# State space operands made in 27 steps between a network's half groups, and u laid out by parts with copies

## The chip, the cores and the metric

The kernel runs on one core of one Trainium2 chip. The metric is the device time of one execution in microseconds; the time before is the median of 3 runs. On this core TensorE (PE) multiplies, VectorE (DVE), ScalarE (ACT) and GpSimd (POOL) work on elements, and SyncE (SP) issues the transfers (DMAs). Each engine takes its instructions in the order in which they stand in its queue.

## The reference, cut to what matters

A sequence of 256 tokens of width 1024 goes through two hybrid layers (a gated delta rule mixer and a gated feed forward network) and then through two layers of another kind, each of three parts: network, token mixer, network. The change lies in the second kind. Its token mixer has a state space branch:

```python
lam_bar = jnp.exp(lam * dt)                          # 32 groups x 64 states, complex
b_bar = ((lam_bar - 1.0) / lam)[..., None] * b
bu = jnp.einsum('blgn,gpn->blgp', uf.astype(jnp.complex64), b_bar)
_, states = lax.associative_scan(combine, (a_all, bu), axis=1)   # state = lam_bar * state + bu
y = jnp.real(jnp.einsum('gnp,blgp->blgn', c, states)) + d_skip * uf
...
def swiglu(h, w_in, w_out):                          # the networks around it
    gate, up = jnp.split(h @ w_in, 2, axis=-1)
    return (jax.nn.silu(gate) * up) @ w_out
```

The kernel doesn't scan token by token. It takes four tokens at a time (SL = 4) and needs, per layer, matrices that depend on the weights alone: the input weights times the powers of lam_bar, the output weights times the powers, their products among the four tokens, and a table of powers. These are the state space operands of the title.

## The kernel before, in words

All tokens stay on the chip and all weights stream in once. Every product is made in three f32 parts: each weight block of 128x1024 is fetched by SP (`wr`, 512 KB, 4 buffers), cast by ACT or by DVE (L232, L234) to `wh` (5 buffers), and DVE subtracts the two to give `wl` (L241, 4 buffers). `wblk` keeps four blocks ahead: while the matmuls of block n are written, the fetch, cast and subtraction of block n + 4 are.

A network (`ffn`) goes through its hidden columns in groups of four tiles of 128 (g0 = 0, 4, ..., 20). Per group there are two half groups, gate and up. Each half group (`group`) is four weight blocks and 96 matmuls of 128x256 in L271; a block holds two of the eight steps of the contraction for all four tiles, so that all four sums open in the first block of the half group and close in its last. The sums lie in the PSUM pool `pg`, which has four banks. An up half group takes over the gate's banks when ACT has made `sg` of them (L432), and the next gate half group takes over the up's banks when DVE has made `act` (L445: the up sum times sg). `act` is then split into `ah` (ACT, L372) and `al` (DVE, L373) for the product with the third matrix. `mod_step` (L493 to L503) is spread over the blocks too: a 512 KB transfer into `mraw` and a DVE multiply (L501).

`ssm_params` (from L1104) makes the state space operands of a layer. Per call: two transfers of 512 KB (`stb`, `sbb`), 48 DVE operations on 128x512 (L1116, L1133) on `scp`, `smi` and `stb`, 32 transposes of 128x128 on PE (L1159) with 8 ACT copies out of PSUM (L1160), 240 small matmuls (L1170) with ACT copies (L1176), and 36 small DVE operations for the table. It is called whole, from the first group of a network (`s.later`, after the up half group of g0 = 0); both calls lie in the networks of the first layer of the second kind, its first and its last. In this text the blocks of the network with the first call are told by half group: gate 0, up 0, gate 1, up 1, gate 2 and so on, four blocks each.

The mixer (`mixer2`) computes u (ACT, L1340), lays it out by its place in the four tokens into `up` with 16 transfers of 32 KB on SP (L1343 to L1345), goes on with the narrow product (PE, L311) and the values, and then `ssm_tile` multiplies `up` by the operands (L1205, L1230).

The queues: nothing reorders the instructions on the chip. The order in which they stand on each engine is set when the program is built, and a change in one place can move others; what it does here is shown with the change.

Of the kernel before, what the change touches and what calls it, by code (L numbers as in the profile page):

```python
# [18 lines left out]
NF = 22  # L19
# [15 lines left out]


SL = 4
NP = T // SL

CI = {"ident": 0, "causal": 1, "upto": 2, "n": 3}  # L40
# [105 lines left out]
class Kern:  # L146
    def __init__(s, nc, tc, ctx, d):
        s.nc, s.tc, s.d = nc, tc, d
        s.blocks, s.made, s.used, s.ready = all_blocks(), 0, 0, []
        s.off = 0  # L150
        s.n = 0
        s.make = s.rest = s.later = None
        s.credit = s.share = s.hshare = 0.0
        s.todo = [(l, j) for l in range(DEPTH) for j in range(72)]
        s.px = s.sc_ = None
        s.next_ssm = 0
        pool = lambda name, bufs, **kw: ctx.enter_context(tc.tile_pool(name=name, bufs=bufs, **kw))
        s.wraw = pool("wraw", 4)
        s.whi = pool('whi', 5)
        s.wlo = pool('wlo', 4)  # L160
        s.const = pool("const", 1)
        s.state = pool("state", 1)
        s.misc = pool("misc", 2)
        s.pg = pool("pg", 4, space=PSUM)
# [249 lines left out]
    def ffn(s, wg, wu, wd, h, done, wg0=0, wu0=0, last=False, then=None):  # L414
        nc, tc = s.nc, s.tc
        rho = h.rho
        with tc.tile_pool(name=s.nm("ffn"), bufs=1, reuse_waits="tile") as pool:
            ah = s.t(pool, [P, NF, T], "ah", F32R)
            al = s.t(pool, [P, NF, T], "al", F32R)
            for g0 in range(0, NF, 4):  # L420
                n = min(4, NF - g0)
                gp = s.group(wg, [wg0 + (g0 + c) * P for c in range(n)], KD, h.h, h.l)
                due = h.due
                if due:
                    h.settle()
                    if then:
                        then()
                sg = []
                for c in range(n):
                    a = s.t(pool, [P, T], "sg", bufs=4)  # L430
                    if not due:
                        nc.scalar.activation(out=a, in_=gp[c][:, :T], func=AF.Silu)  # L432
                    else:
                        nc.vector.tensor_tensor(out=a, in0=gp[c][:, :T], in1=rho, op=ALU.mult)
                        bias = {}
                        if h.shift is not None:
                            cc = s.t(pool, [P, 1], "cc", bufs=4)
                            s.shifted(cc, gp[c])
                            bias = {"bias": cc}
                        nc.scalar.activation(out=a, in_=a, func=AF.Silu, **bias)  # L440
                    sg.append(a)
                up = s.group(wu, [wu0 + (g0 + c) * P for c in range(n)], KD, h.h, h.l)
                for c in range(n):
                    a = s.t(pool, [P, T], "act", bufs=2)
                    nc.vector.tensor_tensor(out=a, in0=up[c][:, :T], in1=sg[c], op=ALU.mult)  # L445
                    s.split(ah[:, g0 + c, :], al[:, g0 + c, :], a)
                if s.later and g0 == 0:
                    s.later(pool, ah[:, 0, 0:1])
                    s.later = None
            s.preload(AF.Sqrt, al[0:1, NF - 1, 0:1])  # L450
            for half in range(2):
                ps = (s.group_by_token if last else s.group)(wd, tiles4(half * 512), NF,
                                                             lambda k: ah[:, k, :], lambda k: al[:, k, :])
                for c in range(len(ps)):
                    if last:
                        done(half, c, ps[c])
                    else:
                        done(half * 4 + c, ps[c][:, :T])
# [71 lines left out]
    def layer2(s, l, z, sq, last=False, subs=(0, 1, 2)):  # L530
        for i in subs:
            if i != 1 and (l if i == 0 else l + 1) == s.next_ssm < DEPTH:
                s.later = lambda pool, after, n=s.next_ssm: s.ssm_params(n, pool, after)
                s.next_ssm += 1
            s.mod_done(l, i)
            gains, weights = s.modA[l][:, i * 8:i * 8 + 8], None
            if sq is None:
# [488 lines left out]
    def ssm_coef(s, pool, after):  # L1026
# [73 lines left out]
        for i in range(2):  # L1100
            tt(lam[:, i, 0:3], r[:, 0:3], cs[:, i], ALU.mult)
            tt(lam[:, i, 3], r[:, 3], pw[:, i, 0], ALU.mult)

    def ssm_params(s, l, pool, after):  # L1104

        nc = s.nc
        V, G, A, PE = nc.vector, nc.gpsimd, nc.scalar, nc.tensor
# [14 lines left out]
        nc.sync.dma_start(out=b, in_=s.d["ssmb"][l].rearrange("p (i j r) -> p i j r", i=2, j=16))  # L1124
        c0, c1 = half(c[:, 0:512]), half(c[:, 512:1024])

        re, im = [[cp[:, i, :, e] for e in range(SL + 1)] for i in range(2)]
        tt(re[0], c0, bc(cr), ALU.mult)
        tt(v, c1, bc(ci), ALU.mult)
# [5 lines left out]
        for e in range(SL):  # L1135
            lr, li = lam[0][e], lam[1][e]
            tt(re[e + 1], re[0], lr, ALU.mult)
            tt(v, im[0], li, ALU.mult)
            tt(re[e + 1], re[e + 1], v, ALU.add)
            tt(im[e + 1], im[0], lr, ALU.mult)  # L1140
            tt(v, re[0], li, ALU.mult)
            tt(im[e + 1], im[e + 1], v, ALU.subtract)

        a = tb.rearrange("p (j i t r) -> p j i t r", j=16, i=2, t=SL)
        for i in range(2):
            A.copy(out=a[:, :, i, SL - 1], in_=b[:, i])
        for e in range(SL - 1):
            lr, li = lam[0][e], lam[1][e]
            ar, ai = a[:, :, 0, SL - 2 - e], a[:, :, 1, SL - 2 - e]
            tt(ar, b[:, 0], lr, ALU.mult)  # L1150
            tt(v, b[:, 1], li, ALU.mult)
            tt(ar, ar, v, ALU.subtract)
            tt(ai, b[:, 1], lr, ALU.mult)
            tt(v, b[:, 0], li, ALU.mult)
            tt(ai, ai, v, ALU.add)
        for j in range(0, 16, 2):
            tp = s.mps()
            for n in range(4):
                PE.transpose(tp[:, n * P:(n + 1) * P], a[:, j + n // 2, n % 2].rearrange("p t r -> p (t r)"), s.ident)  # L1159
            A.copy(out=mi[:, j:j + 2], in_=tp.rearrange("p (j i m) -> p j i m", j=2, i=2))  # L1160

        tz = tb[:, 0:2048].rearrange("p (j t r) -> p j t r", j=16, t=SL)
        for t in range(1, SL):
            G.memset(tz[32 * t:32 * t + 32, :, 0:t], 0.0)
        for j in range(0, 16, 4):
# [8 lines left out]
            for t in range(SL):  # L1174
                rows = slice(32 * t, 32 * t + 32)
                A.copy(out=tz[rows, j:j + 4, t:], in_=p4[rows, :, t:])  # L1176
        tab = tb[:, 2048:].rearrange("p (i j t) -> p i j t", i=2, j=16)
        c, z = tab[:, 0], tab[:, 1]
        G.memset(c[:, :, 0:1], 1.0)
        G.memset(z[:, :, 0:1], 0.0)  # L1180
        for e in range(6):
            m = 1 << e
# [6 lines left out]
            tt(z1, c0, ps, ALU.mult)  # L1189
            tt(v, z0, pc, ALU.mult)  # L1190
            tt(z1, z1, v, ALU.add)
        s.ssmp = mi, cp, tz, c, z

    def ssm_tile(s, l, pool, u, q, done):
# [104 lines left out]
    def mixer2(s, l, h, done):  # L1299
        nc, tc = s.nc, s.tc  # L1300
# [3 lines left out]
        with tc.tile_pool(name=s.nm("m2"), bufs=1, reuse_waits="tile") as pool:  # L1304
# [36 lines left out]
                             bias=cc)  # L1341
            for t in range(SL):
                for jm in range(4):  # L1343
                    nc.sync.dma_start(out=up.rearrange("p (c j) m -> p c j m", j=4)[32 * t:32 * t + 32, :, jm],
                                      in_=u[32 * jm:32 * jm + 32, :, t * NP:(t + 1) * NP])  # L1345
            ps = s.narrow(DEPTH + l)
            s.ahead()
            V.tensor_tensor(out=fb2, in0=ps[:, T:T + 1], in1=s.col(("fb", l)), op=ALU.add)
# [576 lines left out]
```

## Time and profile before

| | before |
|---|---|
| median of 3 runs | 1973.62 us (1973.2 to 1974.64) |
| profiled execution | 1974.74 us, of which span 1972.9 us |
| PE busy | 1880.0 us, 95% |
| DVE busy | 1514.3 us, 77% |
| ACT busy | 1074.0 us, 54% |

The span runs from the first to the last instruction in the profile, and the execution's own time is 1.84 us more. Busy time is counted over the whole span. An idle engine costs time only where the chain that ends last goes through the work it waits for.

### The profile page before, as it was taken

To read this page: it belongs to the slowest core of one execution; us is meant where nothing else is said; L and a number is where in the kernel's file an instruction comes from. 1 tells how busy PE (TensorE), PEld (TensorE's weight loads), DVE (VectorE), ACT (ScalarE), POOL (GpSimd) and SP (SyncE) were. 2 spreads that over 40 slices of the span, in tenths; PEclk is the share of its full clock that TensorE was granted. 3 is DMA by queue.
4 is the path that set the end of the run, shared out by engine and by line. 5 is a ranking of instruction groups with operands and counts; after the bars stand their busy time and mean duration, and the time that the engine had idled before them with its cause. 6 is when DMAs were issued, how large, how long until landed. Compare 5 with 4: busy or idle time off the path is not lost.

```text
span 1972.9 us, 40030 instructions
## 1 busy us (share of the span) xinstructions
PE 1880.0 (95%) x16106; PEld 1825.2 (93%) x16106; DVE 1514.3 (77%) x2826; ACT 1074.0 (54%) x1975; POOL 8.3 (0%) x20
## 2 busy tenths in 40 slices
PE   7999999999999996999999987999999999999998
PEld 6999999999999986998899986999999899999997
DVE  8978887998978698966774898877876677478554
ACT  6766544676644463545555653455544555566443
POOL 0000000000000000000000000000000000000000
PEclk8999999999999998999999998999999999999999
DMA  5434787533777753774343643775677443354553
GB/s 194 139 108 166 273 287 280 177 137 133 237 276 280 270 202 135 282 261 167 118 150 136 218 161 142 264 265 192 237 274 261 161 140 127 142 171 160 180 188 115
DMA packets 110922, 384.83 MB, mean 195 GB/s; under 512 B 16400, under 2 KB 16912, under 8 KB 110736
## 3 DMA queue, kind: packets, MB, share of 16 engines
q1 hardware_dynamic: 110448, 381.88, 55.8%
q8 instruction: 126, 2.06, 0.4%
q14 instruction: 60, 0.49, 0.1%
q10 hardware_dynamic: 288, 0.39, 0.1%
HBM read 380.12 MB, written 1.05 MB: 193 GB/s over the span
## 4 chain that ended last, share of the span: by engine, by line
PE 78%; DVE 11%; ACT 5%; DMA 4%; issue 2%; SPq 0%; DVEq 0%; ACTq 0%
PE g L271 66%; DMA mraw<-in_modw 3%; PE g L291 3%; DVE wl L241 2%; DVE smi L1116 1%; DVE scp L1116 1%; ACT wh L234 1%; DVE stb L1116 1%; DVE mraw L501 1%; PE m L1205 1%; DVE xs L135 1%; PE m L1159 1%; PE m L1170 1%; PE m L848 1%; PE m L853 1%
## 5 line engine op out<-in xcount | busy, mean ns | idle before, releaser
L271 PE MATMUL g<-xh,wh 128*128 128x256 f32 (+1 forms) x3264 | 919.0, 287 | 22.3 <-ACT xh L141 7.9
L271 PE MATMUL g<-xl,wh 128*128 128x256 f32 x3264 | 925.2, 286 | 7.3 <-DVE xl L390 7.3
L271 PE MATMUL g<-xh,wl 128*128 128x256 f32 (+1 forms) x3264 | 913.8, 286 | 2.6 <-DVE wl L241 2.6
L241 DVE TENSOR_TENSOR wl<-wr,wh 128x1024 fp32r<-128x1024 f32 (+1 forms) x576 | 696.7, 1213 | 240.6 <-PE g L271 144.8
L234 ACT CAST wh<-wr 128x1024 fp32r<-128x1024 f32 (+1 forms) x528 | 551.6, 1047 | 510.3 <-PE g L271 306.0
L271 PEld LDWEIGHTS g<-xh,wh 128*128 128x128 f32 x3264 | 617.2, 191 | 30.5 <-ACT xh L141 9.7
L271 PEld LDWEIGHTS g<-xl,wh 128*128 128x128 f32 x3264 | 624.7, 192 | 9.0 <-DVE xl L390 7.9
L271 PEld LDWEIGHTS g<-xh,wl 128*128 128x128 f32 x3264 | 618.7, 192 | 5.1 <-DVE wl L241 3.4
L271 PE MATMUL g<-ah,wl 128*128 128x256 f32 x880 | 246.0, 280 | 0.0
L271 PE MATMUL g<-ah,wh 128*128 128x256 f32 x880 | 245.4, 279 | 0.1
L271 PE MATMUL g<-al,wh 128*128 128x256 f32 x880 | 245.4, 279 | 0.0
L501 DVE SCALAR_TENSOR_TENSOR mraw<-mraw,siluc 128x1024 f32<-128x1024 f32 x144 | 175.8, 1221 | 44.8 <-DMA mraw<-in_modw 44.3
L271 PEld LDWEIGHTS g<-al,wh 128*128 128x128 f32 x880 | 165.5, 188 | 0.0
L271 PEld LDWEIGHTS g<-ah,wl 128*128 128x128 f32 x880 | 165.0, 188 | 0.0
L271 PEld LDWEIGHTS g<-ah,wh 128*128 128x128 f32 x880 | 164.5, 187 | 0.4 <-issue 0.3
L372 ACT CAST ah<-act 128x256 fp32r<-128x256 f32 x132 | 50.7, 405 | 98.8 <-DVE act L445 98.1
L445 DVE TENSOR_TENSOR act<-g,sg 128x256 f32<-128x256 f32 x132 | 53.5, 420 | 12.6 <-PE g L271 7.7
L373 DVE TENSOR_TENSOR al<-act,ah 128x256 fp32r<-128x256 f32 x132 | 53.1, 418 | 11.1 <-ACT ah L372 8.4
L432 ACT ACTIVATE sg<-g 128x256 f32<-128x256 f32 x108 | 39.8, 384 | 38.0 <-PE g L271 38.0
L1159 PE MATMUL m<-cst,stb 128*128 128x128 f32 x64 | 13.1, 373 | 28.5 <-DVE stb L1116 28.5
L1159 PEld LDWEIGHTS m<-cst,stb 128*128 128x128 f32 x64 | 11.2, 197 | 29.5 <-DVE stb L1116 29.5
L271 PE MATMUL g<-gl,wh 128*128 128x256 f32 x128 | 36.0, 281 | 0.0
(453 smaller groups left out, 2122.7 us busy)
## 6 DMA issues: line engine op xcount, KB each, us to landing
wr<-in_wstream SPq DMA_DIRECT2D x568, 512.0 KB, 4.3
mraw<-in_modw SPq DMA_DIRECT2D x144, 512.0 KB, 4.2
wr<-in_wstream SPq DMA_DIRECT2D x8, 256.0 KB, 5.1
stb<-in_ssmc SPq DMA_DIRECT2D x2, 512.0 KB, 3.5
sbb<-in_ssmb SPq DMA_DIRECT2D x2, 512.0 KB, 4.4
up<-u SPq DMA_DIRECT2D x32, 32.0 KB, 1.9
x<-in_x SPq DMA_DIRECT2D x2, 256.0 KB, 5.6
x<-in_x SPq DMA_DIRECT2D x1, 512.0 KB, 7.4
```

The lines of the kernel that those rows point to most:

```text
L135: nc.vector.scalar_tensor_tensor(out=a, in0=s.z[:, k, :], scalar=s.gains[:, k:k + 1], in1=s.rho, op0=ALU.mult, op1=ALU.mult)
L234: nc.scalar.copy(out=hi[:, :n], in_=raw[:, :n])
L241: e.tensor_tensor(out=lo[:, :n], in0=raw[:, :n], in1=hi[:, :n], op=ALU.subtract)
L271: nc.tensor.matmul(ps[c][:, :x.shape[-1]], wt, x, start=(bi == 0 and k == 0 and i == 0), stop=(bi == len(specs) - 1 and k == n - 1 and i = ...
L291: nc.tensor.matmul(ps[h], x(k0 + k)[:, h * P:(h + 1) * P], wt[:, k, :], start=(k0 == 0 and k == 0 and i == 0), stop=(k0 + k == kt - 1 and ...
L372: s.nc.scalar.copy(out=out_h, in_=src)
L373: s.nc.vector.tensor_tensor(out=out_l, in0=src, in1=out_h, op=ALU.subtract)
L432: nc.scalar.activation(out=a, in_=gp[c][:, :T], func=AF.Silu)
L445: nc.vector.tensor_tensor(out=a, in0=up[c][:, :T], in1=sg[c], op=ALU.mult)
L501: nc.vector.scalar_tensor_tensor(out=w, in0=w, scalar=1.0, in1=s.sc_, op0=ALU.mult, op1=ALU.mult, accum_out=s.mod[l][:, j:j + 1])
L1116: tt = lambda o, a, b, op: V.tensor_tensor(out=o, in0=a, in1=b, op=op)
L1159: PE.transpose(tp[:, n * P:(n + 1) * P], a[:, j + n // 2, n % 2].rearrange("p t r -> p (t r)"), s.ident)
```

## The change

`ssm_params` becomes a generator: 26 yields cut it into 27 steps. `s.later` now only starts it; `ssm_steps`, called in `ffn` after each gate half group and after each up half group, writes the next steps into the program, so that 27 steps spread over the eleven half groups from up 0 on: 3, 3, 3, 3, 3, 2, 2, 2, 2, 2, 2. The first step is the two transfers, the second six DVE operations of 128x512, the next fourteen three each, then four steps with 8 transposes each, four with the small matmuls, and the table. The arithmetic is the same. In the mixer the 16 transfers from u to up become 16 copies of 32x256, eight on ACT and eight on DVE.

```diff
--- before.py
+++ after.py
@@ -35,6 +35,7 @@
 
 
 SL = 4
+SSM_STEPS = 27
 NP = T // SL
 
 CI = {"ident": 0, "causal": 1, "upto": 2, "n": 3}
@@ -153,7 +154,7 @@
         s.credit = s.share = s.hshare = 0.0
         s.todo = [(l, j) for l in range(DEPTH) for j in range(72)]
         s.px = s.sc_ = None
-        s.next_ssm = 0
+        s.next_ssm, s.steps = 0, []
         pool = lambda name, bufs, **kw: ctx.enter_context(tc.tile_pool(name=name, bufs=bufs, **kw))
         s.wraw = pool("wraw", 4)
         s.whi = pool('whi', 5)
@@ -425,6 +426,7 @@
                     h.settle()
                     if then:
                         then()
+                s.ssm_steps(2 * ((NF - 1 - g0) // 4) + 1)
                 sg = []
                 for c in range(n):
                     a = s.t(pool, [P, T], "sg", bufs=4)
@@ -447,6 +449,7 @@
                 if s.later and g0 == 0:
                     s.later(pool, ah[:, 0, 0:1])
                     s.later = None
+                s.ssm_steps(2 * ((NF - 1 - g0) // 4))
             s.preload(AF.Sqrt, al[0:1, NF - 1, 0:1])
             for half in range(2):
                 ps = (s.group_by_token if last else s.group)(wd, tiles4(half * 512), NF,
@@ -530,8 +533,7 @@
     def layer2(s, l, z, sq, last=False, subs=(0, 1, 2)):
         for i in subs:
             if i != 1 and (l if i == 0 else l + 1) == s.next_ssm < DEPTH:
-                s.later = lambda pool, after, n=s.next_ssm: s.ssm_params(n, pool, after)
-                s.next_ssm += 1
+                s.later = s.ssm_start
             s.mod_done(l, i)
             gains, weights = s.modA[l][:, i * 8:i * 8 + 8], None
             if sq is None:
@@ -1101,6 +1103,17 @@
             tt(lam[:, i, 0:3], r[:, 0:3], cs[:, i], ALU.mult)
             tt(lam[:, i, 3], r[:, 3], pw[:, i, 0], ALU.mult)
 
+    def ssm_start(s, pool, after):
+        s.steps = list(range(SSM_STEPS))
+        s.work = s.ssm_params(s.next_ssm, pool, after)
+        s.next_ssm += 1
+
+    def ssm_steps(s, rest):
+
+        for _ in range(-(-len(s.steps) // (rest + 1))):
+            s.steps.pop()
+            next(s.work, None)
+
     def ssm_params(s, l, pool, after):
 
 
@@ -1124,6 +1137,7 @@
         nc.sync.dma_start(out=b, in_=s.d["ssmb"][l].rearrange("p (i j r) -> p i j r", i=2, j=16))
         c0, c1 = half(c[:, 0:512]), half(c[:, 512:1024])
 
+        yield
         re, im = [[cp[:, i, :, e] for e in range(SL + 1)] for i in range(2)]
         tt(re[0], c0, bc(cr), ALU.mult)
         tt(v, c1, bc(ci), ALU.mult)
@@ -1137,9 +1151,11 @@
             tt(re[e + 1], re[0], lr, ALU.mult)
             tt(v, im[0], li, ALU.mult)
             tt(re[e + 1], re[e + 1], v, ALU.add)
+            yield
             tt(im[e + 1], im[0], lr, ALU.mult)
             tt(v, re[0], li, ALU.mult)
             tt(im[e + 1], im[e + 1], v, ALU.subtract)
+            yield
 
         a = tb.rearrange("p (j i t r) -> p j i t r", j=16, i=2, t=SL)
         for i in range(2):
@@ -1150,14 +1166,18 @@
             tt(ar, b[:, 0], lr, ALU.mult)
             tt(v, b[:, 1], li, ALU.mult)
             tt(ar, ar, v, ALU.subtract)
+            yield
             tt(ai, b[:, 1], lr, ALU.mult)
             tt(v, b[:, 0], li, ALU.mult)
             tt(ai, ai, v, ALU.add)
+            yield
         for j in range(0, 16, 2):
             tp = s.mps()
             for n in range(4):
                 PE.transpose(tp[:, n * P:(n + 1) * P], a[:, j + n // 2, n % 2].rearrange("p t r -> p (t r)"), s.ident)
             A.copy(out=mi[:, j:j + 2], in_=tp.rearrange("p (j i m) -> p j i m", j=2, i=2))
+            if j % 4:
+                yield
 
         tz = tb[:, 0:2048].rearrange("p (j t r) -> p j t r", j=16, t=SL)
         for t in range(1, SL):
@@ -1174,6 +1194,7 @@
             for t in range(SL):
                 rows = slice(32 * t, 32 * t + 32)
                 A.copy(out=tz[rows, j:j + 4, t:], in_=p4[rows, :, t:])
+            yield
         tab = tb[:, 2048:].rearrange("p (i j t) -> p i j t", i=2, j=16)
         c, z = tab[:, 0], tab[:, 1]
         G.memset(c[:, :, 0:1], 1.0)
@@ -1189,6 +1210,8 @@
             tt(z1, c0, ps, ALU.mult)
             tt(v, z0, pc, ALU.mult)
             tt(z1, z1, v, ALU.add)
+            if e % 2:
+                yield
         s.ssmp = mi, cp, tz, c, z
 
     def ssm_tile(s, l, pool, u, q, done):
@@ -1341,8 +1364,9 @@
                              bias=cc)
             for t in range(SL):
                 for jm in range(4):
-                    nc.sync.dma_start(out=up.rearrange("p (c j) m -> p c j m", j=4)[32 * t:32 * t + 32, :, jm],
-                                      in_=u[32 * jm:32 * jm + 32, :, t * NP:(t + 1) * NP])
+                    e = A.copy if (t + jm) % 2 else V.tensor_copy
+                    e(out=up.rearrange("p (c j) m -> p c j m", j=4)[32 * t:32 * t + 32, :, jm],
+                      in_=u[32 * jm:32 * jm + 32, :, t * NP:(t + 1) * NP])
             ps = s.narrow(DEPTH + l)
             s.ahead()
             V.tensor_tensor(out=fb2, in0=ps[:, T:T + 1], in1=s.col(("fb", l)), op=ALU.add)
```

The order around two places follows. First **DVE, before**, from the fourth block of up 1 (`wl_9964`) to the first block of gate 2 (`wl_10009`). `act_10130` is the first act of up 1, which frees the first bank for gate 2; L1116 are the operations of 128x512.

```order
L1116 TENSOR_TENSOR scp_9571<-scp_9571,smi_9570 128x16x32
L241 TENSOR_TENSOR wl_9964<-wr_9962,wh_9963 128x1024
L1116 TENSOR_TENSOR smi_9570<-scp_9571,ssm_lam 128x512
L1116 TENSOR_TENSOR scp_9571<-scp_9571,ssm_lam 128x16x32
...
L1116 TENSOR_TENSOR stb_9572<-stb_9572,smi_9570 128x16x32
L1116 TENSOR_TENSOR smi_9570<-sbb_9573,ssm_lam 128x512
L1116 TENSOR_TENSOR stb_9572<-sbb_9573,ssm_lam 128x16x32
L1116 TENSOR_TENSOR stb_9572<-stb_9572,smi_9570 128x16x32
L445 TENSOR_TENSOR act_10130<-g_10003,sg_9995 128x256
L241 TENSOR_TENSOR wl_10009<-wr_10007,wh_10008 128x1024
L501 SCALAR_TENSOR_TENSOR mraw_9968,mod_2605<-mraw_9968,siluc 128x1024
L373 TENSOR_TENSOR al_9242<-act_9566,ah_9241 128x256
L445 TENSOR_TENSOR act_10134<-g_10004,sg_9997 128x256
L373 TENSOR_TENSOR al_9242<-act_10130,ah_9241 128x256
```

The 25 operations between wl_9964 and act_10130 are all of L1116; 23 more stand further up, between the blocks of up 1.

**DVE, after**, around the same place: `wl_9743`, `wl_9773` and `wl_9806` belong to the first three blocks of gate 2, `act_9864` is the first act of up 1 and L1129 the operations of 128x512.

```order
L242 TENSOR_TENSOR wl_9743<-wr_9741,wh_9742 128x1024
L1129 TENSOR_TENSOR smi_9570<-scp_9571,ssm_lam 128x512
L1129 TENSOR_TENSOR scp_9571<-scp_9571,ssm_lam 128x16x32
L1129 TENSOR_TENSOR scp_9571<-scp_9571,smi_9570 128x16x32
L242 TENSOR_TENSOR wl_9773<-wr_9771,wh_9772 128x1024
L1129 TENSOR_TENSOR smi_9570<-scp_9571,ssm_lam 128x512
L504 SCALAR_TENSOR_TENSOR mraw_9777,mod_2605<-mraw_9777,siluc 128x1024
L1129 TENSOR_TENSOR scp_9571<-scp_9571,smi_9570 128x16x32
L447 TENSOR_TENSOR act_9864<-g_9737,sg_9729 128x256
L447 TENSOR_TENSOR act_9868<-g_9738,sg_9731 128x256
L242 TENSOR_TENSOR wl_9806<-wr_9804,wh_9805 128x1024
L374 TENSOR_TENSOR al_9242<-act_9864,ah_9241 128x256
```

The acts now stand ahead of the third block's wl, with 21 operations of 128x512 ahead of them (before, all 48); the other 27 come later. In the first network the reciprocal of L614 has also moved, from behind these acts to ahead of the first of the 21.

Behind act_9868 DVE goes on like this: the rest of up 1's acts, and the next operations.

```order
L374 TENSOR_TENSOR al_9242<-act_9868,ah_9241 128x256
L447 TENSOR_TENSOR act_9872<-g_9739,sg_9733 128x256
L242 TENSOR_TENSOR wl_9836<-wr_9834,wh_9835 128x1024
L447 TENSOR_TENSOR act_9876<-g_9740,sg_9735 128x256
L1129 TENSOR_TENSOR scp_9571<-scp_9571,ssm_lam 128x16x32
L1129 TENSOR_TENSOR smi_9570<-scp_9571,ssm_lam 128x512
L374 TENSOR_TENSOR al_9242<-act_9872,ah_9241 128x256
L374 TENSOR_TENSOR al_9242<-act_9876,ah_9241 128x256
L1129 TENSOR_TENSOR scp_9571<-scp_9571,smi_9570 128x16x32
L1129 TENSOR_TENSOR scp_9571<-scp_9571,ssm_lam 128x16x32
L1129 TENSOR_TENSOR smi_9570<-scp_9571,ssm_lam 128x512
L1129 TENSOR_TENSOR scp_9571<-scp_9571,ssm_lam 128x16x32
```

The third and fourth act stand behind one wl each and two splits.

**PE, before**, at the end of up 1 (`g_10003` to `g_10006`) and the start of gate 2 (`g_10146` its first sum):

```order
L271 MATMUL g_10006<-xh_9142,wh_9963 128x256
L271 MATMUL g_10006<-xl_9143,wh_9963 128x256
L271 MATMUL g_10006<-xh_9142,wl_9964 128x256
L1159 MATMUL m_9628<-cst,stb_9572 128x128 x4
L1159 MATMUL m_9634<-cst,stb_9572 128x128 x4
L1159 MATMUL m_9640<-cst,stb_9572 128x128 x4
L271 MATMUL g_10146<-xh_9142,wh_10008 128x256
L1159 MATMUL m_9646<-cst,stb_9572 128x128 x4
L1159 MATMUL m_9652<-cst,stb_9572 128x128 x4
L271 MATMUL g_10146<-xl_9143,wh_10008 128x256
L1159 MATMUL m_9658<-cst,stb_9572 128x128 x4
L1159 MATMUL m_9664<-cst,stb_9572 128x128 x4
```

All 32 transposes stand here, ahead of nearly all of gate 2.

**PE, after**, where the transposes (L1177, the L1159 of before) now stand: in up 3 and the start of gate 4 (`g_10352` to `g_10355`).

```order
L272 MATMUL g_10352<-xh_9142,wh_10228 128x256
L272 MATMUL g_10352<-xl_9143,wh_10228 128x256
L272 MATMUL g_10353<-xh_9142,wh_10228 128x256
L1177 MATMUL m_10320<-cst,stb_9572 128x128 x3
L1177 MATMUL m_10326<-cst,stb_9572 128x128 x4
L1177 MATMUL m_10332<-cst,stb_9572 128x128 x4
L272 MATMUL g_10352<-xh_9142,wl_10229 128x256
L1177 MATMUL m_10338<-cst,stb_9572 128x128 x4
L272 MATMUL g_10352<-xh_9142,wh_10228 128x256
L272 MATMUL g_10352<-xl_9143,wh_10228 128x256
L272 MATMUL g_10352<-xh_9142,wl_10229 128x256
```

The transposes have moved from directly behind up 1 to some 14 blocks later. On SP the only difference is that the two groups of 16 transfers `up<-u` are gone.

## Rows read from the trace of the kernel before

**Rows 1.** The page's head and its first part: busy time, share, instructions.

```profile
span 1972.9 us, 40030 instructions
...
PE 1880.0 (95%) x16106; PEld 1825.2 (93%) x16106; DVE 1514.3 (77%) x2826; ACT 1074.0 (54%) x1975; POOL 8.3 (0%) x20
```

**Rows 2.** Waits of PE by line and releaser: total, times, longest, us.

```profile
PE m L1159 <- DVE stb L1116: 28.5, 4, 12.7
```

**Rows 3.** Timeline of PE, first call: start, length, instruction, [idle before <-releaser].

```profile
749.98 0.28 PE L271 MATMUL g<-xh,wl 128*128 128x256 f32 x1
762.96 0.48 PE L1159 MATMUL m<-cst,stb 128*128 128x128 f32 x1 [12.70 <-DVE stb L1116]
...
778.42 0.38 PE L271 MATMUL g<-xh,wl 128*128 128x256 f32 x1
```

**Rows 4.** Timeline of PE, second call.

```profile
1188.51 0.28 PE L271 MATMUL g<-xh,wl 128*128 128x256 f32 x1
...
1217.92 0.38 PE L271 MATMUL g<-xl,wh 128*128 128x256 f32 x1
```

**Rows 5.** PE by line, 749.9 to 778.4 us.

```profile
L1170 PE MATMUL m<-scp,sbb 128*32 128x128 f32 (+3 forms) x240 | 6.9, 241 | 0.6 <-ACT stb L1176 0.6
L1159 PE MATMUL m<-cst,stb 128*128 128x128 f32 x32 | 6.1, 355 | 14.3 <-DVE stb L1116 14.3
```

**Rows 6.** Windows: each engine's busy us (instructions), TensorE's clock, DMA share, GB/s.

```profile
726.00:750.00 24.00, 23.21 (x194) 22.91 (x193) 23.96 (x39) 9.23 (x15) 0.00 (x0) 1.00 0.56 208
750.00:760.00 10.00, 0.26 (x3) 0.06 (x1) 9.69 (x15) 0.00 (x0) 0.00 (x0) 0.76 0.00 0
780.00:920.00 140.00, 140.00 (x1185) 140.00 (x1185) 104.82 (x166) 66.79 (x94) 0.00 (x0) 1.00 0.73 255
1163.00:1188.00 25.00, 23.88 (x199) 23.61 (x199) 24.88 (x41) 9.95 (x16) 0.00 (x0) 1.00 0.58 211
```

**Rows 7.** Timeline of DVE, first call.

```profile
728.44 0.68 DVE L1116 TENSOR_TENSOR scp<-stb,ssm_cr 128x512 f32<-128x512 f32 x1
729.04 0.68 DVE L1116 TENSOR_TENSOR smi<-stb,ssm_ci 128x512 f32<-128x512 f32 x1
...
764.26 0.69 DVE L1116 TENSOR_TENSOR stb<-stb,smi 128x512 f32<-128x512 f32 x1
764.87 0.42 DVE L445 TENSOR_TENSOR act<-g,sg 128x256 f32<-128x256 f32 x1
765.21 1.21 DVE L241 TENSOR_TENSOR wl<-wr,wh 128x1024 fp32r<-128x1024 f32 x1
766.34 1.22 DVE L501 SCALAR_TENSOR_TENSOR mraw<-mraw,siluc 128x1024 f32<-128x1024 f32 x1
```

**Rows 8.** Timeline of DVE, second call.

```profile
1166.84 0.68 DVE L1116 TENSOR_TENSOR scp<-stb,ssm_cr 128x512 f32<-128x512 f32 x1
...
1203.38 0.42 DVE L445 TENSOR_TENSOR act<-g,sg 128x256 f32<-128x256 f32 x1
```

**Rows 9.** DVE by line and shape: the reciprocal of the norm.

```profile
L612 DVE RECIPROCAL r<-sd 128x256 f32<-128x256 f32 x6 | 10.5, 1744 | 0.0
```

**Rows 10.** Timeline of PE at the start of the first mixer: two other waits.

```profile
932.11 0.39 PE L271 MATMUL g<-xl,wh 128*128 128x256 f32 x1 [3.72 <-DVE xl L390]
...
946.93 1.07 PE L311 MATMUL g<-z,sqb 128*32 128x256 f32 x16 [2.21 <-DVE xs L1339]
```

**Rows 11.** Windows there, columns as in rows 6.

```profile
930.00:940.00 10.00, 7.89 (x40) 7.89 (x41) 5.62 (x17) 5.69 (x11) 0.62 (x2) 0.66 0.00 1
940.00:950.00 10.00, 7.05 (x63) 5.95 (x61) 8.89 (x25) 6.68 (x12) 0.00 (x0) 1.00 0.01 2
950.00:963.00 13.00, 13.00 (x123) 12.83 (x124) 7.91 (x20) 5.25 (x10) 0.00 (x0) 1.00 0.34 81
```

**Rows 12.** Timeline of SP's DMA queue: the transfers of u in the first mixer.

```profile
949.58 10.57 SPq L1344 DMA_DIRECT2D up<-u  x16
```

**Rows 13.** One tile's instructions (`up`), times ns: who reads it, and when first.

```profile
L1205 PE MATMUL m<-up,smi x128: 217/275/324, 963.1 to 1657.1; 128*128 128x64 f32 x128
```

**Rows 14.** ACT by line and shape: the copies out of PSUM.

```profile
L1176 ACT COPY stb<-m 32x256 f32<-32x256 f32 x8 | 2.9, 363 | 0.1
```

## The prediction

> **What bounds the kernel now.** The first part of the page gives PE 1880.0 us of a span of 1972.9 [rows 1]: the kernel is bound by PE, and what can be won without taking work from PE is the time in which PE waits, some 93 us. So the second view is the list of PE's waits. Its longest row is this change's subject: the transposes L1159 waited 28.5 us in all for the DVE operations L1116 [rows 2]. The third is PE's timeline at both calls: the last matmul of up 1 starts at 749.98, the first transpose at 762.96 after 12.70 us of waiting, and the even run of matmuls is there again at 778.42 [rows 3]; in the second call the same lies between 1188.51 and 1217.92 [rows 4]. In the windows PE has 0.26 us of work from 750 to 760, while DVE is busy for 9.69 of 10 us, so DVE's queue is what ends the wait. Farther on, from 780 to 920, PE is busy for 140.00 of 140 us and DVE for 104.82 [rows 6]: there DVE could take a quarter more, and PE would not notice. The question is how much of the DVE work gets there.
>
> **What a call costs before.** PE's full rate is 140.00 us for 1185 matmuls [rows 6], 0.118 us each. First call: from 750.10 (749.98 and one matmul) to 778.42 are 28.3 us. Of that, work that stays is the 240 small matmuls, 6.9 us, the 32 transposes, 3.8 at full rate (in the stall they took 6.1 [rows 5]), and five matmuls of gate 2 that stand between, 0.6: together 11.3. Lost are 17.0. To that comes what PE lost in up 0 and up 1, when wl came late behind L1116: 24.00 less 23.21, 0.8. Second call: 29.3 us less 11.9 (ten matmuls of gate 2 stand between) is 17.4, and 25.00 less 23.88, 1.1 [rows 6]. In all 17.8 + 18.5 = 36.3 us. That is the most that the steps can give.
>
> **What a call costs after.** The 48 operations don't vanish, and the spreading is not even: the order has 21 of them between the splits of up 0 and the first act of up 1, 17 more before the first act of up 2, and 10 behind that. PE does not wait for stb any more at the end of up 1, since the transposes stand 12 to 16 blocks later. But gate 2 needs a PSUM bank, which that act frees. When does the act come?
> DVE starts on the 21 at 728.44. Ahead of the act stand 21 x 0.60 us (the spacing of the first two) = 12.6; six wl at 1.13 (765.21 to 766.34) = 6.8; three mraw of the same shape = 3.4 [rows 7]; and in the first network the reciprocal, 1.74 [rows 9]. That makes 24.5: the act starts at 752.9 and ends, with its 0.42, at 753.4. PE, no longer late by 0.8, is there at 749.3: it waits 4.1 us. The second act follows 0.34 later; the third stands behind a wl and two splits (1.13 + 0.68), the fourth behind another wl. They end at 753.7, 755.8 and 757.3. Gate 2's first block does six matmuls (0.71 us) per bank, so it ends at 757.3 + 0.7 = 758.0 in place of 749.3 + 24 x 0.118 = 752.1. **Gate 2 costs 5.9.**
> Gate 3: up to the first act of up 2 stand, by the order, 17 operations (10.2), five wl (5.7), two mraw (2.3) and two splits (0.7), together 18.9: that act ends at about 776.5. PE gets there at 758.0 + 7 blocks of 2.83 = 777.8, so it doesn't wait for the first; but the third and fourth acts stand behind mraw, wl and splits, and end at about 779.7 and 782.1, where PE wants them at 779.2 and 780.4. **Gate 3 costs 2.1.** Behind it 10 operations are left, 6 us, beside a quarter of DVE's time free: nothing.
> The second call has no reciprocal: 1166.84 [rows 8] + 22.8 + 0.42 = 1190.1, and PE arrives at 1188.63 - 1.1 = 1187.5. It waits 2.6, the banks add 1.8, gate 3 again 2.1: 6.5. Both calls: 8.0 + 6.5 = 14.5.
>
> **The clock after the wait.** PE's granted clock can fall after a wait. At the first mixer a wait of 3.72 us [rows 10] is followed by a window with the clock at 0.66 [rows 11]: 6.8 of its 10 us at the lower of the two levels, 1.2 GHz, which loses 3.4 us. A wait of 2.21 us is followed by 1.00. The new waits, 4.1 and 2.6, lie on both sides. If PE is late by 3.4, it no longer waits at gate 3, so the first call pays 1.3 more; for the second I take half, 0.7. Together 2.0; the bounds are 0 and 6.8.
> The Trainium skill ("TensorE: Matmul & The Clock Gate", section "HAM oscillation — how this bites in real kernels") says that matmuls that run in bursts with waits between fall back to the half clock and pay for it anew at each wait. The rows agree for the longer wait and show nothing for the shorter. [...]
>
> **Transposes and small matmuls** now stand among matmuls of up 3 and behind. They still wait for ACT to empty PSUM; before that was 0.6 us in a call [rows 5]. ACT has the time (66.79 of 140 us busy [rows 6]), but PE takes its queue in order. Bounds 0 and 2 a call; I take 1, so 2.0.
>
> **The copies of u.** SP spends 10.57 us on the 16 transfers [rows 12], and the first reader of up is at 963.1 [rows 13]. In between PE is busy for 13.00 of 13.00 us [rows 11], with the values' matmuls: the transfers are hidden, and removing them gives 0. In their place ACT has eight copies of 32x256; the same shape from PSUM takes 0.363 [rows 14], so 2.9 us. DVE has eight that are at most as long as a 128x256 act, 0.34: 2.7. On ACT what waits behind them are fx's and the values' evictions, with PE's product beside them. If that cover holds they cost nothing, if not 2.9 a mixer. PE already waited 2.21 us for this chain just ahead [rows 10], so the cover is thin: I take a third, 0.9, twice 1.8.
> The Trainium skill speaks for more ("DMA: Bandwidth & Descriptors", section "Rules for kernel authors"): transfers under 64 KB are mostly overhead. The row of SP agrees, 0.66 us for each 32 KB, but it is overhead beside a busy PE. By the rule the sum would gain up to 21 us; by the rows nothing.
>
> **The sum.** 36.3 - 14.5 - 2.0 - 2.0 - 1.8 = 16.0 us. The profiled execution took 1974.74, so 1958.7; it lay 1.1 above the median of the runs, so **1958** in runs. The rest of the program's order shifts a little too; for that I take 0, give or take 3.
> Bounds: if the banks, the clock, PSUM and the copies cost nothing, the waits 4.1 + 2.6 remain, and the gain is 29.6 (1944). If all bounds fall on the bad side, the calls cost 14.5 + 6.8 + 4, the copies 5.8, and the gain is 5.2 (1968).
>
> **Rivals.**
> *All is hidden.* DVE's share in up 0 and up 1 turns out smaller, because operations that don't wait for PE start earlier than 728.44, and the act is in time. Gain up to 36.3: 1937. For it: PE waited only 0.8 there. Against: DVE was busy for 23.96 of 24.00 us [rows 6], so there is nothing to close up. 0.10.
> *The transfers do count.* By the rule of the skill named above, which has its price in the sum by row: twice 10.57 us besides, 1937 too. Against it is PE's 13.00 of 13.00. 0.02.
> *The wait only moves.* Each gate boundary that has 17 or 21 operations ahead of it pays the full price: wait, banks and clock, 5.9 + 3.4 = 9.3 us. With two of them, gate 2 and gate 3, that is 18.6 against 18.2 before: no change, 1973. Against: by the count the act of up 2 is in time by 1.3 us; a slip of DVE by 3 us (a late mraw, operations 0.72 apart where one needs the other's result) would turn it. 0.12.
> *Slower.* The same with a third boundary, gate 4, because DVE never catches up: 27.9 - 18.2 = 9.7 a call, 1993. It decides from the second boundary at full price on. Against: between two boundaries PE needs 8 x 2.83 = 22.7 us, and DVE has eight wl, eight acts and splits and three mraw, 9.0 + 2.7 + 3.4 = 15.1; 7.6 remain, 12 operations' worth, and behind gate 3 only 10 come. 0.10.
>
> **How the numbers follow.** The case of the sum, with its own range of 1944 to 1968, has 0.66. The cases at 1937 have 0.12, no change 0.12, slower 0.10. About 0.2%, 3.9 us, is what a measurement of this kernel can tell from no change. So faster 0.78, same 0.12, slower 0.10. The range goes from 1941, which leaves most of the cases at 1937 out, to 1971, into the case without change.
>
> **What would show it.** Right: no wait of the transposes for stb; in its place PE waits at the start of gate 2, near 749 and 1187, 3 to 5 and 2 to 3 us, for the act (its line), and then by turns under a microsecond or two for the next banks; a lower clock behind the first of them; DVE full up to that act; the transposes tens of us later without a wait above 1 us; the mixer with PE busy from 950 to 963 as before and no transfers of u. Wrong: a wait of over 4 us at gate 3 or gate 4, PE waiting in the mixers for ACT, or the first act of up 1 in time for gate 2.

## The result, and the profile after

The changed kernel takes 1947.19 us, median of 4 runs (1946.6 to 1951.95), beside 1974.12 for the kernel before (by now four runs): a ratio of 0.9869 with an interval of 0.9852 to 0.9886, so 1.1% to 1.5% faster. The forecast was 1958, with a range of 1941 to 1971.

The page of the kernel after, its head and first part, answers to [rows 1]:

```profile
span 1945.1 us, 40024 instructions
...
PE 1874.2 (96%) x16106; PEld 1820.2 (94%) x16106; DVE 1510.7 (78%) x2842; ACT 1075.2 (55%) x1989; POOL 8.3 (0%) x20
```

The span is 27.8 us shorter with the same matmuls. In the list of PE's waits of the kernel after, the row of [rows 2] is gone. Its place has:

```profile
PE g L272 <- DVE act L447: 8.6, 2, 5.3
```

Two waits, for the act (DVE's product that frees a bank), not for stb. PE's timeline of the kernel after shows where: at the start of gate 2, in the first and in the second call (compare [rows 3, 4]).

```profile
749.94 0.28 PE L272 MATMUL g<-xh,wl 128*128 128x256 f32 x1
755.49 0.55 PE L272 MATMUL g<-xh,wh 128*128 128x256 f32 x1 [5.27 <-DVE act L447]
755.84 0.41 PE L272 MATMUL g<-xl,wh 128*128 128x256 f32 x1
...
758.75 0.28 PE L272 MATMUL g<-xh,wh 128*128 128x256 f32 x1
...
1175.70 0.28 PE L272 MATMUL g<-xh,wl 128*128 128x256 f32 x1
1179.27 0.55 PE L272 MATMUL g<-xh,wh 128*128 128x256 f32 x1 [3.29 <-DVE act L447]
...
1185.36 0.28 PE L272 MATMUL g<-xl,wh 128*128 128x256 f32 x1
```

Behind each wait the matmuls run at the lower clock for a while (0.41 us long in place of 0.28): 15 of them from 755.49 to 758.75, 3.3 us where 15 x 0.118 = 1.8 would do, so 1.5 lost; 28 from 1179.27 to 1185.36, 2.8 lost. DVE's timeline of the kernel after, up to the acts of up 1 in the first call (compare [rows 7]); the last two rows are the first acts of up 2 in each call:

```profile
730.30 1.74 DVE L614 RECIPROCAL r<-sd 128x256 f32<-128x256 f32 x1
731.96 0.62 DVE L1129 TENSOR_TENSOR scp<-stb,ssm_cr 128x512 f32<-128x512 f32 x1
...
754.92 0.75 DVE L447 TENSOR_TENSOR act<-g,sg 128x256 f32<-128x256 f32 x2
755.59 1.22 DVE L242 TENSOR_TENSOR wl<-wr,wh 128x1024 fp32r<-128x1024 f32 x1
756.72 0.76 DVE L374 TENSOR_TENSOR al<-act,ah 128x256 fp32r<-128x256 f32 x2
757.39 0.42 DVE L447 TENSOR_TENSOR act<-g,sg 128x256 f32<-128x256 f32 x1
...
778.50 0.75 DVE L447 TENSOR_TENSOR act<-g,sg 128x256 f32<-128x256 f32 x2
...
1202.86 0.42 DVE L447 TENSOR_TENSOR act<-g,sg 128x256 f32<-128x256 f32 x1 [0.80 <-PE g L272]
```

From the reciprocal to the act are 24.6 us; the forecast had 24.5. The windows of the kernel after (columns as in [rows 6]):

```profile
726.00:750.00 24.00, 24.00 (x203) 23.88 (x201) 23.95 (x37) 10.16 (x16) 0.00 (x0) 1.00 0.70 248
750.00:760.00 10.00, 4.73 (x28) 4.55 (x28) 10.00 (x18) 4.59 (x7) 0.00 (x0) 0.83 0.79 299
760.00:780.00 20.00, 20.00 (x170) 20.00 (x170) 19.75 (x30) 7.11 (x10) 0.00 (x0) 1.00 0.51 182
```

In gate 1 and up 1 PE has no gap any more; between 750 and 760 it has 4.73 us of work where it had 0.26; then it doesn't stop again before the third product, not at gate 3 either, whose first matmul starts at 779.77. The first act of up 2 ends 0.9 us earlier, at 778.92; in the second call DVE even waits 0.80 us for PE there.

**The stretches.** To compare kernels, PE's matmuls of weight blocks are counted through and two stretches of 36 blocks timed, each between the same two matmuls by count: from the start of gate 1 to the start of the third product (the last gate and the last up have two blocks each). All transposes of a call lie in it, and 236 to 256 of its 256 small matmuls. At full rate a stretch takes 864 x 0.118 + 6.9 + 3.8 = 112.8 us. "Rest" is the span without the two.

| kernel | first | second | rest | span |
|---|---|---|---|---|
| before | 131.7 | 132.6 | 1708.6 | 1972.9 |
| after | 121.6 | 120.7 | 1702.9 | 1945.1 |
| after, once more | 122.3 | 118.5 | 1705.0 | 1945.8 |
| copies alone | 132.0 | 131.0 | 1708.5 | 1971.5 |
| steps alone | 121.8 | 119.5 | 1703.0 | 1944.3 |
| 13 ahead of the act | 117.2 | 116.4 | 1705.5 | 1939.1 |
| 15 ahead | 116.9 | 116.2 | 1705.5 | 1938.6 |
| 18 ahead | 118.1 | 119.6 | 1709.7 | 1947.4 |
| 29 ahead | 124.9 | 124.9 | 1712.4 | 1962.2 |
| after, mraw held | 120.5 | 120.5 | 1703.6 | 1944.6 |
| 15 ahead, mraw held | 123.4 | 122.9 | 1701.6 | 1947.9 |

The stretches hold 22.1 us of the 27.8. The rest gives 5.7. Each row is one execution and not a median: with 15 ahead it is the shortest of that kernel's runs, with 29 ahead and with 15 ahead and mraw held the longest of theirs.

### The profile page after: what moved, and what is told of

The parts are those of the page before. It is cut to its first block, busy times and chain, and to the rows that moved or that the text cites. A ratio compares the mean times of both kernels' runs of the same rounds, so it can differ in the third digit from the quotient of the medians.

```text
span 1945.1 us, 40024 instructions
## 1 busy us (share of the span) xinstructions
PE 1874.2 (96%) x16106; PEld 1820.2 (94%) x16106; DVE 1510.7 (78%) x2842; ACT 1075.2 (55%) x1989; POOL 8.3 (0%) x20
## 4 chain that ended last, share of the span: by engine, by line
PE 80%; DVE 9%; ACT 6%; DMA 3%; issue 2%; SPq 0%; DVEq 0%; ACTq 0%
PE g L272 68%; PE g L292 3%; DVE wl L242 2%; DMA mraw<-in_modw 1%; ACT wh L235 1%; DMA wr<-in_wstream 1%; PE m L1190 1%; PE m L1228 1%; DVE mraw L504 1%; PE m L855 1%; DVE scp L1129 1%; DVE sqa L335 1%; PE m L850 0%; DVE cv L711 0%; PE m L1316 0%
## 5 line engine op out<-in xcount | busy, mean ns | idle before, releaser
L272 PE MATMUL g<-v,wl 128*128 128x256 f32 x128 | 35.9, 281 | 0.0
L272 PE MATMUL g<-v,wh 128*128 128x256 f32 x128 | 35.8, 280 | 0.0
```

What stands on the lines that cost most here:

```text
L272: nc.tensor.matmul(ps[c][:, :x.shape[-1]], wt, x, start=(bi == 0 and k == 0 and i == 0), stop=(bi == len(specs) - 1 and k == n - 1 and i = ...
```

## Experiments

The theory: the gain is the steps', and what is left of the loss is the place of the first act of up 1 in DVE's queue, whatever stands ahead of it. The main rivals: the transfers that were removed cost time; the wait only moves on.

**Copies alone.** The kernel before with

```diff
-                    nc.sync.dma_start(out=up..., in_=u...)
+                    e = A.copy if (t + jm) % 2 else V.tensor_copy
+                    e(out=up..., in_=u...)
```

> Only the copies of u in place of the 16 transfers per mixer; the operands are made whole, as before. Theory (the gain is the steps'; the transfers were hidden): the waits of the transposes for stb stay at 28.5 us, and the time is 1968 to 1975, that is before less at most the 3.9 us by which the two mixers were shorter in the changed kernel's trace. Rival (the transfers of 32 KB cost time by themselves): at least 8 us faster, 1966 or less, with the mixers shorter by 4 us or more each.

1975.17 us (11 runs) beside 1974.34: ratio 1.0006, interval 0.9996 to 1.0016. That is 0.2 us above what was expected, and the rival, a gain of at least 8 us, is out: 32 copies in place of the 32 transfers gain at most 0.8 us and lose at most 3.2. The waits are as they were:

```profile
PE m L1159 <- DVE stb L1116: 28.5, 4, 12.7
```

**Steps alone.** The kernel after, with the 16 transfers per mixer put back in place of the copies.

> Only the 27 steps; the 16 transfers per mixer stay. Theory: two waits for the act at gate 2 of 5.3 and 3.3 us, as in the changed kernel, and 1948 to 1952. Rival (the transfers cost time): 1955 or more, with PE waiting for something in the mixers that it doesn't wait for in the changed kernel.

1947.54 us, ratio 0.9872, interval 0.9857 to 0.9888, as the whole change within its interval (0.5 us under the range that was expected). The waits for the act are the same to a tenth:

```profile
PE g L272 <- DVE act L447: 8.6, 2, 5.3
```

**Fewer and more operations ahead of the act.** Only the share of the half groups in the 27 steps changes:

```diff
-SSM_STEPS = 27
+SSM_STEPS, SSM_DUE = 27, (1, 2, 2, 3, 3, 3, 3, 3, 3, 2, 2)
...
-        for _ in range(-(-len(s.steps) // (rest + 1))):
+        for _ in range(SSM_DUE[10 - rest] if s.steps else 0):
```

> The changed kernel, but the 27 steps are dealt out to the eleven half groups as 1, 2, 2, 3, 3, 3, 3, 3, 3, 2, 2 in place of 3, 3, 3, 3, 3, 2, ...: 13 operations of 128x512 stand ahead of the first act of up 1 in place of 21, and the reciprocal of the first network behind. Theory (what is left is the act's place in DVE's queue): the act starts 6 to 8 us earlier, before PE gets to gate 2 in both calls; the waits of 5.3 and 3.3 and the slow stretches behind them (1.5 and 2.7) go, and the time is 1934 to 1938. Rival (DVE is the bound of these groups, the wait only moves to gate 3 or 4): the same act waits there, and 1943 to 1949.

> The changed kernel with the steps dealt out as 5, 4, 3, 3, 2, 2, 2, 2, 2, 1, 1: 29 operations of 128x512 ahead of the first act of up 1 in place of 21, the reciprocal behind it. Theory: the act is later by 8 x 0.60 = 4.8 us and one wl or mraw more, less 1.7 in the first call: waits of 8 to 10 and 8 to 9 us in place of 5.3 and 3.3, 1953 to 1959. Rival (PE's wait is set by something else than the number of operations ahead of the act): 1945 to 1949.

With 13 ahead: 1941.14 us, ratio 0.9833, interval 0.9819 to 0.9847; no wait for the act in either call. Its windows around both places:

```profile
750.00:770.00 20.00, 20.00 (x170) 20.00 (x170) 19.62 (x30) 9.66 (x13) 0.00 (x0) 1.00 0.68 242
1180.00:1200.00 20.00, 20.00 (x168) 19.83 (x167) 19.55 (x29) 8.15 (x13) 0.00 (x0) 1.00 0.75 275
```

The time is 3 us above the range that was expected. The stretches got 8.7 us shorter, not the 12.9 that the waits and the lower clock had cost. Of the 4.2 that are missing, 2.1 are waits of the transposes, one in each call, for the operations that were put off (the row below). The rest is 2.7 us longer than after the change. So the theory holds for the wait, and missed what follows it.

```profile
PE m L1177 <- DVE stb L1129: 2.1, 2, 1.1
```

With 29 ahead: 1960.09 us, ratio 0.9937 (0.9923 to 0.995), one us above the range. The waits grow as the count does (the first a little less than worked out), in PE's timeline of that kernel:

```profile
760.01 0.55 PE L272 MATMUL g<-xh,wh 128*128 128x256 f32 x1 [7.52 <-DVE act L447]
...
1193.68 0.55 PE L272 MATMUL g<-xh,wh 128*128 128x256 f32 x1 [8.47 <-DVE act L447]
```

**The changed program once more**, for how well a stage repeats.

> The changed kernel's program once more (the same instructions in the same order on every engine; only the function that deals out the steps is written with a table). It tells how well a stage's time repeats. Theory: 1946 to 1951, the waits for the act at gate 2 again 5.3 and 3.3 us within 0.2, and the mixers within 1 us of the first profile. Rival (stages of the mixers vary by 2 to 3 us from one execution to the next, so that the 2.6 and 1.6 us by which they were shorter after the change say nothing): mixers that differ by over 1.5 us between the two profiles of one program.

1947.49 us, ratio 0.9862 (0.9845 to 0.988). The waits at gate 2 are 5.4 and 3.3 again. Twenty blocks from the start of the first mixer on, between the same two matmuls, took 86.7 us here and 85.4 in the first profile, 1.3 apart where within 1 was expected; so a difference of that size in a mixer tells nothing. The second stretch took 118.5 and 120.7. The difference there is the clock: the same wait as above is followed by full speed (the window behind it). And at full speed PE comes to gate 3 too early for its act, by 0.23 us. PE's timeline, first and second call:

```profile
756.99 0.55 PE L272 MATMUL g<-xh,wh 128*128 128x256 f32 x1 [5.42 <-DVE act L447]
...
760.06 0.28 PE L272 MATMUL g<-xh,wl 128*128 128x256 f32 x1
...
1181.54 0.36 PE L272 MATMUL g<-xh,wh 128*128 128x256 f32 x1 [3.29 <-DVE act L447]
...
1204.81 0.35 PE L272 MATMUL g<-xh,wh 128*128 128x256 f32 x1 [0.23 <-DVE act L447]
```

```profile
1180.00:1190.00 10.00, 8.46 (x71) 8.49 (x72) 10.00 (x20) 4.61 (x7) 0.00 (x0) 1.00 0.44 159
```

**18 and 15 operations ahead.** The same edit with (3, 2, 3, 3, 3, 3, 2, ...) and (2, 2, 3, 3, 3, 3, 3, 2, ...).

> The changed kernel with the steps dealt out as 3, 2, 3, 3, 3, 3, 2, ...: 18 operations of 128x512, seven wl and three mraw ahead of the first act of up 1, the reciprocal behind it: 10.8 + 7.9 + 3.4 = 22.1 us behind the last split of up 0, in place of 24.6 and 22.9. Theory: the wait for the act at gate 2 is 2.3 to 2.8 us in the first call and 2.2 to 2.7 in the second, and the time is between the two neighbours, 1942 to 1946. Rival (the waits of the later banks and at gate 3, 1.8 and 2.1 us by the prediction, were only hidden by the slow clock and come out where the first wait is short): waits for the act at more than one place in each call, and 1946 to 1950.

> The changed kernel with the steps dealt out as 2, 2, 3, 3, 3, 3, 3, 2, ...: 15 operations, six wl and three mraw ahead of the act, the reciprocal behind it: 9.0 + 6.8 + 3.4 = 19.2 us, so the act ends about 0.5 us before PE gets to gate 2. The transposes stand earlier than with 13 operations. Theory: no wait for the act at gate 2 or gate 3, no wait of the transposes for stb, 1935 to 1940, as fast as the kernel with 13 or up to 4 us faster. Rival (some other wait comes at gate 3, since more operations stand before it): a wait there of over 1.5 us, and 1941 to 1945.

With 18: 1947.8 us, ratio 0.986 (0.9845 to 0.9875), no faster than the change itself: a miss, and a time in the range that was given to the rival. The waits at gate 2 were near what was expected, one in each call, and in the first call a third wait came at gate 3, as the rival has it; in the second call it did not. PE's timeline of that kernel:

```profile
753.80 0.35 PE L272 MATMUL g<-xh,wh 128*128 128x256 f32 x1 [2.75 <-DVE act L447]
...
777.80 0.36 PE L272 MATMUL g<-xh,wh 128*128 128x256 f32 x1 [0.96 <-DVE act L447]
...
1180.30 0.55 PE L272 MATMUL g<-xh,wh 128*128 128x256 f32 x1 [2.97 <-DVE act L447]
```

Only the wait of 2.97 was followed by a lower clock (its windows):

```profile
750.00:760.00 10.00, 7.25 (x61) 7.07 (x61) 10.00 (x19) 5.64 (x8) 0.00 (x0) 1.00 0.69 239
1180.00:1190.00 10.00, 9.70 (x58) 9.73 (x59) 10.00 (x19) 4.13 (x7) 0.00 (x0) 0.68 0.41 152
```

The stretches are 4.6 us shorter than after the change, and the rest 6.8 longer, in parts that the edit doesn't touch; why is open. With 15: 1943.1 us, ratio 0.9837 (0.9819 to 0.9854), not to be told from 13. It is 3 us above what was expected, in the range of its rival, a wait of over 1.5 us at gate 3. There was no wait at gate 2, but there were two small ones at gate 3 in each call, together 1.3 us, somewhat less than the rival has. The first call:

```profile
773.81 0.35 PE L272 MATMUL g<-xh,wh 128*128 128x256 f32 x1 [0.82 <-DVE act L447]
...
776.33 0.39 PE L272 MATMUL g<-xh,wh 128*128 128x256 f32 x1 [0.51 <-DVE act L447]
```

**The modulation held back.** DVE time of another kind is taken from ahead of the act:

```diff
-        while s.credit >= 1 and s.todo:
+        if s.credit >= 1 and s.todo and not 17 < len(s.steps) < 27:
```

> The changed kernel with its own share of steps, but the modulation's transfers and multiplies (mraw, L504 of the changed kernel) are held back from the first steps until ten have been written, and come one per block afterwards. Ahead of the first act of up 1 stand 20 operations of 128x512, seven wl and no mraw, in place of 21, six and three: 12.0 + 7.9, with the reciprocal 1.74 in the first call, so 21.7 and 19.9 us in place of 24.6 and 22.9. Theory (any DVE time ahead of the act counts, of whatever operation): waits for the act at gate 2 of about 2.4 and 0.3 us in place of 5.3 and 3.3, 1940 to 1945. Rival (the state space operations themselves hold PE up, for instance by the bandwidth that both take from the same memory): waits unchanged, 1946 to 1950.

> The kernel with 15 operations ahead of the act, and the modulation held back in the same way: 15 operations, six or seven wl, no mraw, 16 to 17 us (18 in the first call, with the reciprocal), 2 to 4 us before PE gets to gate 2. Theory: no wait at gate 2; the held multiplies come behind it, ahead of the acts of up 2, so there may be waits of 1 to 2 us at gate 3; 1938 to 1944, no clear difference from the kernel with 15 operations. Rival (the mraw multiplies are what DVE lacks time for in these groups): 1934 or less.

The changed kernel with it: the wait at gate 2 is 2.2 us in the first call, as worked out (PE's timeline), and 0.4 in the second. Below it, two rows of PE's waits in that kernel, and one of the kernel with 15 operations and the same hold.

```profile
755.98 0.35 PE L272 MATMUL g<-xh,wh 128*128 128x256 f32 x1 [2.19 <-DVE act L447]
```

```profile
PE g L272 <- DVE wl L242: 5.0, 5, 2.0
PE g L272 <- DVE act L447: 3.2, 3, 2.2
```

```profile
PE g L272 <- DVE wl L242: 6.9, 4, 3.1
```

So any DVE time ahead of the act counts. But the time is 1946.47, 1.5 us above the range. The kernel before took 1977.88 beside it, so only the ratio compares: 0.985 (0.9832 to 0.9869), which can't be told from that of the change. The multiplies that were held come one per block later, and there PE waits for wl, 5.0 us. With 15 operations the hold makes no clear difference, as was expected: 1945.58, ratio 0.9846 (0.9829 to 0.9864). The time is 1.6 us above its range, and PE waits 6.9 us for wl. Here the wait did move.

## Why the prediction was right, and where its sum was off

**The mechanism was right in the main.** The transposes' 28.5 us went, and the act of up 1 took their place at the start of gate 2 in both calls. The waits are 0.3 us above the sizes that were named as the sign, 3 to 5 and 2 to 3. The series of kernels shows that it is the DVE time ahead of the act: none at gate 2 with 13 and 15 operations, 2.8 and 3.0 us with 18, 5.3 and 3.3 with 21 (and the reciprocal in the first call), 7.5 and 8.5 with 29, and 2.2 and 0.4 where the three multiplies are taken out.

**The sum was too small**: 16.0 us against 26.9 in the medians and 27.8 in the spans. That the time lies in the range is in part luck. Of the 11.8 us between sum and spans, 4.3 are the calls, 1.8 the copies and 5.7 the rest of the kernel, for which the sum had 0. In the calls, two charges that didn't come (the later banks and gate 3, 7.8 us) outweighed others that were too small by 6.0. By its terms:
- *What a call costs before*: 36.3 worked out; by the stretches 131.7 + 132.6 - 2 x 112.8 = 38.7. (The 24 us from 726 on, in which wl came late, are gate 1 and up 1 by the count of blocks, not up 0 and up 1; the loss of 0.8 is as it was read.)
- *The wait at gate 2*: 4.1 and 2.6 worked out, 5.27 and 3.29 measured. DVE's time is as computed, 24.6 for 24.5; the start in the first call was not. The reciprocal starts at 730.30, 1.9 us later than the 728.44 taken from [rows 7], while PE got to gate 2 only 0.8 later.
- *The later banks*, 1.8 a call: nothing. This is the step that failed outright. PE was taken to want the four banks in turn within a block. The order of the program after has nine matmuls of the second block (`wh_9772`, `wl_9773`) on the first two banks ahead of the first on the third, `g_9891`:

```
L272 MATMUL g_9890<-xh_9142,wl_9743 128x256
L272 MATMUL g_9889<-xh_9142,wh_9772 128x256
...
L272 MATMUL g_9890<-xl_9143,wh_9772 128x256
L272 MATMUL g_9890<-xh_9142,wl_9773 128x256
L272 MATMUL g_9891<-xh_9142,wh_9742 128x256
```

  So at full rate the third bank is wanted 21 x 0.118 = 2.5 us behind the first, at 757.97, and the third act ends at 757.81. In the second call of the repeated run PE didn't wait for it at full clock either.
- *Gate 3*, 2.1 a call: PE busy 20.00 of 20 us. The first act of up 2 is in time by 0.9 us in the first call (1.3 by the sum), which is less than the 1.5 that PE had just lost at the lower clock. In the repeat, where the second call kept the full clock, PE waited 0.23 there; with 18 ahead 0.96, in one call; with 15 ahead, where PE comes some 6 us earlier, 1.3 in each.
- *The clock*, 2.0 for both: 1.5 + 2.8 = 4.3 in this profile; in the repeat 14 matmuls in 3.1 us, 1.4 lost, behind the first wait and nothing behind the second. Both are within the bounds that were given.
- *Transposes and small matmuls*, 1 a call: what remains of the stretches after the waits and the clock, 121.6 - 112.8 - 5.3 - 1.5 = 2.0 and 120.7 - 112.8 - 3.3 - 2.8 = 1.8. In each call 1.3 us of it are fourteen weight matmuls that stand next to a transpose or a small matmul: from their start to the next one's are 0.20 to 0.23 us in place of 0.118. Two of them, the first and the third row (PE's timeline of the kernel after):

```profile
1234.97 0.28 PE L272 MATMUL g<-xl,wh 128*128 128x256 f32 x1
1235.18 0.63 PE L1190 MATMUL m<-scp,sbb 128*32 128x32 f32 x12
1235.74 0.39 PE L272 MATMUL g<-xh,wl 128*128 128x256 f32 x1
1235.96 0.28 PE L272 MATMUL g<-xh,wh 128*128 128x256 f32 x1
```

Costs after: 18.5 forecast, 16.7 measured; gain of the calls 17.8 forecast, 22.1 measured.
- *The copies of u*, 1.8: the copies-alone ratio allows a loss of 3.2 us and a gain of 0.8, so the term is neither confirmed nor excluded. In the kernel after the copies took 404 ns on ACT and 284 on DVE (363 and at most 340 were taken), by line and shape:

```profile
L1368 ACT COPY up<-u 32x256 f32<-32x256 f32 x16 | 6.5, 404 | 0.2
...
L1368 DVE COPY up<-u 32x256 f32<-32x256 f32 x16 | 4.5, 284 | 0.2
```

- *The rest of the order*, 0 give or take 3: 5.7 us gained, and this **stays open**. In the kernels with steps the rest lies between 1701.6 and 1712.4, and the program that was run twice differs by 2.2 there. The edits may shift the order in other layers too, and the moments at which the clock falls; no run takes these apart.

**The rivals.** That all is hidden (1937) is out: DVE was busy for 23.95 of the 24.00 us, and the act was 5.3 us late. That the transfers count is out by the copies alone. The Trainium skill's rule that a transfer under 64 KB is mostly overhead ("DMA: Bandwidth & Descriptors", section "Rules for kernel authors") is not contradicted, as SP did spend 0.66 us on each [rows 12], but here it is no time of the kernel. That the wait moves on to gate 3 at full price didn't happen, and neither did the slower case: the act of up 2 was in time, though by less than the count against it said. The kernels with mraw held show that the mechanism exists, with wl in place of the act.

## What to carry to other kernels

Work that is spread over a stream should be spread by the load of the queue that it goes into, not by equal counts. Here DVE had no time free ahead of the first act: 21 operations ahead of it cost 8.6 us of waits and, in that profile, 4.3 at the lower clock; with 13 or 15 that went, 2 to 3 us of other waits came, and the medians fell by 4 to 6 us (with 15 the interval still touches that of the change). To predict such a change, count in the built order what stands ahead of the one instruction that the waiting engine needs, price it from the trace, and do the same count on the waiting engine: when it wants the thing is a matter of its order too. Transfers that end before their reader is free can go without a gain that one can measure, as those of u did.

## What the runs showed of the hardware that was not expected

The same wait of 3.29 us in the same program was followed by 6.1 us at the lower clock (1.2 GHz) in one execution and by a granted clock of 1.00 in the other; waits of 2.75 and 2.97 us in one execution were followed by 1.00 and 0.68, and one of 5.27 by only 3.3 us at the lower level. In these rows the length of a wait alone does not tell what the clock takes behind it; half a chance and the full price, as taken in the sum for the second call, is as near as they allow. A copy of 32x256 that moves data to other partitions took 0.404 us on ACT and 0.284 on DVE, whereas ACT's copy of that shape out of PSUM took 0.363 [rows 14].
